# Sums of q's squares by column-group products, the last values turned a unit later, and selection matrices made in the unit before

## The chip, the cores and the metric

The kernel runs on one core of a Trainium2 chip. The metric is the time on the device in microseconds (us), lower is better. A core has TensorE (PE; its weight loads are listed as PEld), VectorE (DVE), ScalarE (ACT), GpSimd (POOL) and SyncE (SP), which here issues most transfers. Each engine works through its own instructions in order; where one needs a result of another engine it waits on a semaphore, and everything behind it on that engine waits with it.

## The reference

A trunk of two layers over 512 positions and 1024 channels in float32. Layer 0 mixes by a gated DeltaNet (8 heads of 128), layer 1 by a Conformer convolution; each layer then attends to a memory of 256 rows and goes through a squared-ReLU MLP. The parts that matter here:

```python
def l2_normalize(x):
    return x * lax.rsqrt(jnp.sum(x * x, axis=-1, keepdims=True) + 1e-6)

def gated_deltanet(h, w_in, w_conv, a_log, dt_bias, out_norm, w_out):
    proj = h @ w_in
    qkv = jax.nn.silu(causal_depthwise_conv(qkv, w_conv))   # q, k, v of 8 heads
    ...
    q = l2_normalize(q) * (DN_HEAD_DIM ** -0.5)
    k = l2_normalize(k)
    ...
    o = chunk_gated_delta_rule(q, k, v, g, beta)
    o = o * lax.rsqrt(jnp.mean(o * o, axis=-1, keepdims=True) + RMS_EPS) * out_norm
    o = o * jax.nn.silu(z)
    return o @ w_out

def conformer_conv(h, w_pw1, b_pw1, w_dw, b_dw, ln_g, ln_b, w_pw2, b_pw2):
    u = h @ w_pw1 + b_pw1
    u = u[..., :D_MODEL] * jax.nn.sigmoid(u[..., D_MODEL:])
    c = causal_depthwise_conv(u, w_dw) + b_dw
    c = jax.nn.silu(layer_norm(c, ln_g, ln_b))
    return c @ w_pw2 + b_pw2
```

For each head and position the sum of q's 128 squares is needed. It enters only in the normalization of the output, so it may come late.

## The kernel before

Activations lie with 128 channels on the partitions and 512 positions along the row. A float32 weight is held as a rounded high part and a rest: ScalarE casts the loaded `raw` to `wh` (L253), VectorE subtracts to get `wl` (L73), and a product is three matmuls (L300 to L302: wh with xh, wh with xl, wl with xh). A projection tile of 128 output channels and 512 positions is 24 matmuls.

The DeltaNet part is written as a row of units: `mains` has the projections, two units for a tile, in the order k, q, z, v of heads 0 to 3 (group 0), then the same of heads 4 to 7 (group 1), then the keys and values of the memory (K and V in the names). Beside it stands a table: `S.at(unit, rank, f, ...)` puts the work f into a unit, and ranks order the work of one unit. Tables at the end of the file give the units: `Q3` for q's squares of each head, `FS` for the recursion on X. The framework's scheduler makes each engine's order from these instructions as they are written out, so a change of a table moves instructions of several engines against each other.

Names in the profile: `h` is a projection's PSUM tile; v0 to v7 in the text are the tiles of the eight heads' values. `cv` is VectorE's copy of such a tile out of PSUM (scaled by `rb`), `cva` the result of the short convolution; q of head h ends as such a `cva` in `QT[h]`, 128 channels x 512 positions. `X` and `fst` are the steps of the recursion that inverts the triangular matrices, all on VectorE, with widths such as 9x23 = 207; it ends with a 32x32 transpose of X to `UB`, copies from UB to `u` and transposes of u to `x`. `mss` and `msd` belong to the memory's norm.

The sums of q's squares: `q3` (L671, L674) turns q of one head by four TensorE transposes into PSUM (`qt`), so that positions lie on the partitions, and ScalarE squares each 128x128 block with a running sum into one column of `ssq` (an ACTIVATE and a READ_ACCUMULATOR each); `norm_q` then adds epsilon.

The values: `v2` turns the values of a group by transposes (`vt`, L818). In group 1, heads 0 to 2 are turned in one unit and head 3 in the next.

The Conformer: `mlp7` (the MLP of layer 0) ends with the residual sums `h`, from which the next norm takes high and low parts `xh` (ACT) and `xl` (DVE) and squares `sq`, summed on GpSimd and VectorE in two accumulators. The conformer's first products `pw` use xh and xl; `ssq` there is the sum of the squares by a product with ones, issued in unit `STAT` of the pw loop. VectorE makes three selection matrices `sel` (L1420 to L1422) at the conformer's start.

Of the kernel before, what the change touches and what calls it, by code (L numbers as in the profile page):

```python
# [10 lines left out]
AF = mybir.ActivationFunctionType  # L11
ALU = mybir.AluOpType
AX = mybir.AxisListType

P = 128
NT = 512
NTAP = 4
PH = 16
KT = 8
EPS = 1e-6  # L20
# [18 lines left out]
def tile_trunk(ctx, tc, xT, memT, x_d, mem_d, prm_d, adt_d, bdw_d, tap_d, fin_d, first_d, w_ab, w_kq, w_v, w_z, w_dno, w_pw1, w_pw2,  # L39
               w_q, w_k, w_vv, w_o, w_up, w_dn, yT):  # L40
    nc = tc.nc
    pe, act, dve, pool = nc.tensor, nc.scalar, nc.vector, nc.gpsimd
# [15 lines left out]
    def slot(dt=F32, s="u", shape=(P, NT)):  # L58
        return up.tile(list(shape), dt, tag="u", name=nm(s))

    def psum(s="ps"):
        return psp.tile([P, NT], F32, tag="ps", name=nm(s))
# [4 lines left out]
    def const(shape, s, dt=F32):  # L67
        return cp.tile(list(shape), dt, tag=s, name=s)
# [3 lines left out]
    def tt(e, o, a, b, op):  # L72
        r = e.tensor_tensor(out=o, in0=a, in1=b, op=op)  # L73
        if e is pool:
            last_pool[:] = [r]
        return r
# [4 lines left out]
    def ts(e, o, a, s1, op0, s2=None, op1=None):  # L81
        if op1 is None:
            return e.tensor_scalar(out=o, in0=a, scalar1=s1, scalar2=None, op0=op0)
        return e.tensor_scalar(out=o, in0=a, scalar1=s1, scalar2=s2, op0=op0, op1=op1)

    def c4(t):
        return t.rearrange("p (c i) -> p c i", c=4)
# [4 lines left out]
    def over_c(t, n=4):  # L92
        return t.unsqueeze(1).to_broadcast([P, n, t.shape[1]])
# [18 lines left out]
    def piece(e, i):  # L112
        e.dma_start(out=raw0[:, i * 256:(i + 1) * 256], in_=w_kq[0][:, i * 256:(i + 1) * 256])
# [11 lines left out]
    ident = const([P, P], "ident")  # L125
# [4 lines left out]
    for i in range(WARM):  # L130
# [5 lines left out]
    pool.affine_select(out=tri_gt, in_=ones, pattern=[[-1, P]], compare_op=ALU.is_gt, fill=0.0,  # L136
                       base=0, channel_multiplier=1)
    piece(act, 1)
    ones_r = const([P, P], "ones_r", F32R)
    pool.tensor_copy(ones_r, ones)  # L140
    tri_mid = const([P, P], "tri_mid")
# [58 lines left out]
    for kind, gq in DN_ORDER:  # L200
        for i in range(2):
            j = gq * 2 + i
# [202 lines left out]

    class Norm:
        def __init__(self, gname):
            self.g, self.acc, self.xs, self.n, self.side = gname, None, [], 0, None

        def add(self, t, h):  # L410
            self.parts(t, h)
# [6 lines left out]
            pin(stt(xl, h, pc(self.g, t), xh.bitcast(F32), ALU.mult, ALU.subtract))  # L418
            self.xs.append((xh, xl))

        def square(self, h, e=pool, side=False):
            sq = slot(s="sq")
            act.activation(sq, h, AF.Square)  # L423
            self.n += 1
            if side:
                if self.side:
                    tt(pool, self.side, self.side, sq, ALU.add)
                self.side = self.side or sq
                return
            if self.acc is None:  # L430
                self.acc = sq
            else:
                tt(dve if self.n == KT else e, self.acc, self.acc, sq, ALU.add)
            if self.n == KT:
                if self.side:
                    tt(dve, self.acc, self.acc, self.side, ALU.add)
                self.hl = split(self.acc, "sq")

        def stat(self):
# [28 lines left out]
    class DeltaNet:  # L468
# [196 lines left out]
            self.QT[h] = qT  # L665

        def q3(self, h):
            ps, sq = psum("qt"), slot(s="sqq")
            for c in range(4):
                cs = slice(c * P, (c + 1) * P)  # L670
                pe.transpose(ps[:, cs], self.QT[h][:, cs], ident)  # L671
            for c in range(4):
                cs = slice(c * P, (c + 1) * P)
                act.activation(sq[:, cs], ps[:, cs], AF.Square, accum_out=self.ssq[:, 4 * h + c:4 * h + c + 1])  # L674

        def norm_q(self, gq):
            v = self.ssq[:, 16 * gq:16 * gq + 16]
            ts(dve, v, v, EPS, ALU.add, EPS * P, ALU.mult)


        def fs_in(self, h):
# [291 lines left out]
    def mem_gain(layer, half):  # L973
        gn = f"xa_mem{layer}"
        if half == 0:
            mem["xs"] = []
        for j in (2 * half, 2 * half + 1):
            if layer == 1:
                m = mem["m"][j].rearrange("p (k t) -> p k t", k=2)
                tt(dve, m, m, over_c(mem["rs"][:, 0:256], 2), ALU.mult)  # L980
            mh = slot(F32R, "mh")
            ml = slot(F32R, "ml")
            for i in range(2):
                ks = slice(i * 256, (i + 1) * 256)
                src = mem["m"][j][:, ks]
                g = pc(gn, 2 * j + i)
                act.activation(mh[:, ks], src, AF.Copy, scale=g)
                stt(ml[:, ks], src, g, mh[:, ks].bitcast(F32), ALU.mult, ALU.subtract)
                mem["xs"].append((mh[:, ks], ml[:, ks]))
# [176 lines left out]
    def mlp7(layer, norm, hres, nxt=None, mid=None):  # L1166
# [123 lines left out]
        new = [None] * 8  # L1290

        def outs(tiles):
            todo = [(n, c, i) for n in range(2) for c in range(2) for i in tiles]
            pss = {i: psum("hT") for i in tiles}
            for n, c, i in todo:
                j = 2 * n + c
                pe.transpose(pss[i][:, j * P:(j + 1) * P], acc[n, 1 - i // 4, c][:, i % 4 * P:i % 4 * P + P], ident)
            for k, i in enumerate(tiles):
                hn = slot(s="h")
                tt(dve, hn, pss[i], hres[i], ALU.add)  # L1300
                new[i] = hn
                if k:
                    nxt.parts(i - 1, new[i - 1])
                if i > 5:
                    nxt.square(new[i - 2], side=True)
            nxt.parts(i, hn)
            for hn in new[0:4] if i == 3 else new[6:8]:
                nxt.square(hn, pool if i == 3 else dve)

        def final(n, m, c, held=None):  # L1310
            opens = n not in fin or fin[n][4][c] is None
# [62 lines left out]
        for g in range(4):  # L1374
            ops, us = [{} for _ in range(4)], []
            for i in range(8):
                w = wnext(("up", layer, g * 4 + i // 2), i % 2)
                ps = psum("up")
# [25 lines left out]
    def taps(m, *pieces):  # L1404
        TAPS.setdefault(m, [])
        for i in pieces:
            t = slot(s="tap")
            nc.sync.dma_start(out=t, in_=tap_d[m - NTAP, i])
            TAPS[m].append(t)

    def conformer(norm, hres, nxt, rest):
        xs = norm.xs
        st, x16 = {}, {}
# [2 lines left out]
        Yp = [fsp.tile([P, 1024], F32, tag="fs", name=nm("cyp")) for _ in range(2)]  # L1416
        bias = slot(s="bdw")[:, 0:P]
        nc.sync.dma_start(out=bias, in_=bdw_d)
        sel = slot(s="sel")
        dve.tensor_reduce(out=sel[:, 128:160], in_=ident.rearrange("p (g t) -> p t g", g=4), op=ALU.add, axis=AX.X)  # L1420
        dve.tensor_reduce(out=sel[:, 160:164], in_=c4(ident), op=ALU.add, axis=AX.X)
        dve.tensor_copy(c4(sel[:, 0:128]), over_c(sel[:, 128:160]))  # L1422
        own, same_t = over_c(sel[:, 160:164]), sel[:, 0:128]

        def pw_mm(i, hf):
# [242 lines left out]
        new = []  # L1668
# [4 lines left out]
        for m in range(8):  # L1673
            w, ps = pss[m] if m in pss else (wnext(("pw2", m // 2), m % 2), psum("pw2"))
            proj(w, ss, ps, 4 if m in pss else 0)
            hn = slot(s="h")
# [13 lines left out]
    for i in range(4):  # L1690
        s = slice(i * 256, (i + 1) * 256)
# [30 lines left out]
    D = DeltaNet(n0)  # L1722
    D.decay_const(0)
    mains, S = [], Sides()
# [70 lines left out]
    for gq in range(2):  # L1795
        f0, nf = FS[gq]
        S.at(f0, 5, D.fs_begin, gq)
        for i in range(nf):
            S.at(f0 + i, 6, D.fs_steps, gq, i * 31 // nf, (i + 1) * 31 // nf)
        S.at(f0 + nf, 1, D.fs_end, gq)  # L1800
        for h in range(4 * gq, 4 * gq + 4):
            S.at(f0 + nf, 1, D.mg_a, h)
        S.at(f0 + 1, 7, D.norm_k, gq)
        S.at(f0 + nf + 2, 7, D.norm_q, gq)
        for i in range(4):
            h = 4 * gq + i
            S.at(f0 + nf - 4 + i, 5, D.mg_pre, h)
        a, b = (4 * gq, 4 * gq + 1), (4 * gq + 2, 4 * gq + 3)
        for j, (f, x, y) in enumerate(((D.mg_wy, a, ()), (D.mg_wy, b, a), (D.mg_te, a, ()), (D.mg_te, b, a), (D.mg_te, (), b))):
            S.at(MG[gq] + j, 1, f, x, y)  # L1810
        S.at(MG[gq] + 2, 1, D.mg_wy, (), b)
        for j, x in ((1, a), (2, b)):
            S.at(MG[gq] + j, 1.5, D.mg_u, x)
        for c in range(4):
            u = at["v", 4 * gq + 3] + V2[gq]
            if gq == 1:
                S.at(u, 3, D.v2, gq, c, (0, 1, 2))
                S.at(u + 1, 0, D.v2, gq, c, (3,))
        n = 0
        for c in range(4):  # L1820
            for step in range(3):
                S.at(REC[gq] + n, 0, D.rec, gq, c, step)
                n += 1
            S.at(REC[gq] + n + (c < 3 if gq == 1 else -(c == 1)), 5, D.o_gate, gq, c)
        S.at(ONORM[gq], 1, D.o_norm, gq)
    S.at(MSQ - 4, 7, mem_tok)
    for j in range(4):
        S.at(MSQ + j, 7, mem_square, j)
# [33 lines left out]
    h = []  # L1862
# [12 lines left out]
    n2 = Norm("mlp_norm0")  # L1875
    h = xattn(0, n1, h, n2)
    n3 = Norm("cv_norm")
    h, rest = mlp7(0, n2, h, n3, lambda: (mem_gain(1, 0), mem_gain(1, 1), taps(NTAP, *range(9))))
    n4 = Norm("xa_norm1")
    h = conformer(n3, h, n4, rest)  # L1880
    n5 = Norm("mlp_norm1")
# [3 lines left out]
    mlp7(1, n5, h)  # L1885


NSLOT = 69
NCV = 6
NRAW = 3  # L1890
RAWB = 6
# [21 lines left out]
ROOT_K = (32, 72)  # L1913
K2 = (15, 16, 18, 19, 45, 46, 49, 48)
Q2 = (18, 20, 22, 23, 48, 50, 50, 53)
Q3 = (24, 25, 27, 29, 55, 56, 57, 59)
FS = ((22, 9), (52, 8))
MG = (36, 68)
V2 = (10, 9)
# [6 lines left out]
TAPK = {0: 8, 1: 9, 2: 11, 3: 12}  # L1926
TAPQ = {0: 12, 4: 44}
TAPV = (37, 38, 39, 40, 69, 69, 70, 71)
STAT = 2
TAPS_U = (4,) * 7 + (6,) * 9 + (3,) * 8 + (0,) * 8  # L1930
TAPS_C = {4: 0, 5: 0, 6: 0, 7: 0}
SHARE = 5
# [113 lines left out]
```

## Time and profile before

| what | us |
|---|---|
| median of 3 runs (1444.5 to 1446.05) | 1444.7 |
| the profiled execution | 1444.54 |
| its span | 1442.8 |
| PE busy | 1432.4 |
| DVE busy | 1053.5 |
| ACT busy | 763.6 |
| POOL busy | 249.2 |

The profiled execution takes 1.7 us more than its span, which runs from its first to its last instruction. The core's mean granted TensorE clock was 0.999. A row of a timeline has the start in us, the duration in us, engine, line, operation, output and inputs, and in brackets the engine's idle time before it and what released it. TensorE's durations are modelled, and neighbours overlap: what a matmul costs the stream is the distance between the starts.

### The profile page before, as it was taken

The page shows a single profiled execution, that of the slowest core. Times are in us where ns is not written, and L with a number is a line of the kernel's source. Part 1 is how long each engine was busy: PE and PEld are TensorE (multiplying, and loading weights), DVE is VectorE, ACT ScalarE, POOL GpSimd, SP SyncE. Part 2 cuts the span into 40 slices and gives each one's busy share as a digit, 9 for nine tenths or more (in the row PEclk, how much of TensorE's full clock was granted, in tenths as well). Part 3 has the DMA queues.
Part 4 walks back from the last instruction along what each step waited for, and adds up shares of the span by engine and source line. Part 5 has one row for each costly group of instructions (what it writes and reads, how often), then busy time and mean ns, then how long its engine had stood idle before and what let it go on. Part 6 is the DMA issues. An engine that isn't in the chain of part 4 may idle for free.

```text
span 1442.8 us, 20243 instructions
## 1 busy us (share of the span) xinstructions
PE 1432.4 (99%) x7670; PEld 1199.2 (83%) x7670; DVE 1053.5 (73%) x1600; ACT 763.6 (53%) x1322; POOL 249.2 (17%) x250
## 2 busy tenths in 40 slices
PE   9999999999999999999999999999999999999998
PEld 7888889888888888888888778888888888888886
DVE  6989888867555765767679899975555766767677
ACT  6767856655444454434355655564444544444354
POOL 1301200102113010010100478111112010010101
PEclk9999999999999999999999999999999999999999
DMA  8232225522214576575766448743215476675853
GB/s 300 73 117 75 70 92 162 195 84 88 74 40 127 153 177 175 141 206 131 198 165 217 141 147 244 252 139 99 73 49 141 117 182 169 149 206 135 222 150 88
DMA packets 71857, 207.80 MB, mean 144 GB/s; under 512 B 15440, under 2 KB 16592, under 8 KB 71760
## 3 DMA queue, kind: packets, MB, share of 16 engines
q1 hardware_dynamic: 60960, 169.22, 35.9%
q0 software_dynamic: 9792, 35.66, 14.5%
q10 hardware_dynamic: 1008, 1.64, 0.3%
q8 instruction: 60, 0.98, 0.3%
q14 instruction: 37, 0.30, 0.1%
HBM read 203.28 MB, written 3.21 MB: 143 GB/s over the span
## 4 chain that ended last, share of the span: by engine, by line
PE 91%; DVE 5%; ACT 2%; issue 1%; DMA 0%; POOL 0%; SPq 0%; DVEq 0%; ACTq 0%; POOLq 0%
PE up L302 8%; PE up L301 8%; PE up L300 8%; PE dn L1218 7%; PE dn L1217 7%; PE dn L1216 7%; PE h L300 3%; PE h L302 3%; PE h L301 3%; PE xo L301 2%; PE q L301 2%; PE xo L300 2%; PE q L300 2%; PE q L302 2%; PE xo L302 2%; PE pw L302 2%
## 5 line engine op out<-in xcount | busy, mean ns | idle before, releaser
L253 ACT CAST wh<-raw 128x1024 fp32r<-128x1024 f32 x259 | 271.6, 1051 | 345.0 <-issue 89.1
L73 DVE TENSOR_TENSOR wl<-raw,wh 128x1024 fp32r<-128x1024 f32 (+1 forms) x250 | 306.0, 1225 | 97.1 <-ACT wh L253 94.8
L300 PE MATMUL up<-xh,wh 128*128 128x512 f32 x512 | 199.7, 390 | 0.0
L302 PE MATMUL up<-xh,wl 128*128 128x512 f32 x512 | 199.3, 389 | 0.0
L301 PE MATMUL up<-xl,wh 128*128 128x512 f32 x512 | 199.2, 389 | 0.0
L302 PEld LDWEIGHTS up<-xh,wl 128*128 128x128 f32 x512 | 96.1, 188 | 19.9
L300 PEld LDWEIGHTS up<-xh,wh 128*128 128x128 f32 x512 | 96.1, 188 | 19.9
L301 PEld LDWEIGHTS up<-xl,wh 128*128 128x128 f32 x512 | 96.1, 188 | 19.9
L241 POOL DMA_DIRECT2D t<-w_dn x48 | 42.1, 914 | 367.5 <-DVE wl L73 269.6
L1216 PE MATMUL dn<-wh,ah 128*128 128x512 f32 (+1 forms) x260 | 100.5, 387 | 0.0
L1218 PE MATMUL dn<-wl,ah 128*128 128x512 f32 (+1 forms) x260 | 100.4, 386 | 0.0
L1217 PE MATMUL dn<-wh,al 128*128 128x512 f32 (+1 forms) x260 | 100.4, 386 | 0.0
L79 DVE SCALAR_TENSOR_TENSOR rl<-up,rb 128x512 f32<-128x512 f32 x64 | 44.1, 689 | 58.4 <-PE up L302 58.4
L253 ACT CAST wh<-t 128x1024 fp32r<-128x1024 f32 x44 | 46.4, 1054 | 55.0 <-PE dn L1217 43.7
L73 DVE TENSOR_TENSOR wl<-t,wh 128x1024 fp32r<-128x1024 f32 x44 | 53.6, 1223 | 28.7 <-ACT wh L253 28.6
L73 POOL TENSOR_TENSOR sq<-sq,sq 128x512 f32<-128x512 f32 x28 | 46.0, 1643 | 154.2 <-ACT sq L423 143.6
L1495 DVE SCALAR_TENSOR_TENSOR ca<-xn,prm,ca 128x512 f32<-128x512 f32 x85 | 64.1, 754 | 5.7 <-ACT ca L1492 3.4
L73 DVE TENSOR_TENSOR acc<-acc,dn 128x512 f32<-128x512 f32 x99 | 66.6, 682 | 1.0
L300 PE MATMUL h<-xh,wh 128*128 128x512 f32 x160 | 64.2, 401 | 0.0
L302 PE MATMUL h<-xh,wl 128*128 128x512 f32 x160 | 62.5, 390 | 0.0
L301 PE MATMUL h<-xl,wh 128*128 128x512 f32 x160 | 62.4, 390 | 0.0
L73 DVE TENSOR_TENSOR al<-u,ah 128x512 fp32r<-128x512 f32 x64 | 44.1, 688 | 21.4 <-ACT ah L359 21.4
(421 smaller groups left out, 3520.2 us busy)
## 6 DMA issues: line engine op xcount, KB each, us to landing
raw<-w_dn SPq DMA_DIRECT2D x68, 512.0 KB, 4.5
raw<-w_up SPq DMA_DIRECT2D x64, 512.0 KB, 4.8
t<-w_dn POOLq DMA_DIRECT2D x48, 512.0 KB, 6.4
tap<-tap SPq DMA_DIRECT2D x48, 256.0 KB, 6.2
raw<-w_pw SPq DMA_DIRECT2D x24, 512.0 KB, 4.6
raw<-w_dn POOLq DMA_DIRECT2D x20, 512.0 KB, 6.6
raw<-w_k SPq DMA_DIRECT2D x16, 512.0 KB, 4.1
raw<-w_vv SPq DMA_DIRECT2D x16, 512.0 KB, 6.1
```

Of the source, the lines that this page charges most:

```text
L73: r = e.tensor_tensor(out=o, in0=a, in1=b, op=op)
L79: return dve.scalar_tensor_tensor(out=o, in0=a, scalar=s, in1=b, op0=op0, op1=op1)
L241: nc.gpsimd.dma_start(out=t, in_=a, accum_op=ALU.add)
L253: ins = [act.copy(h, raw)]
L300: pe.matmul(ps, wh, xh, start=first, stop=False)
L301: pe.matmul(ps, wh, xl, start=False, stop=False)
L302: pe.matmul(ps, wl, xh, start=False, stop=last)
L1216: pe.matmul(ps, xh, w[0][:, s], start=opens and k == 0, stop=False, skip_group_check=True)
L1217: pe.matmul(ps, xl, w[0][:, s], start=False, stop=False, skip_group_check=True)
L1218: pe.matmul(ps, xh, w[1][:, s], start=False, stop=k == 3, skip_group_check=True)
L1495: first["tap"] = dve.scalar_tensor_tensor(out=a, in0=src, scalar=w, in1=a, op0=ALU.mult, op1=ALU.add)
```

## The change

Four edits.

1. **q's squares.** `q3` now only squares q of a head on ScalarE, 128x512 at once, without turning it. `q_sums` multiplies the squares of the four heads of a group by a constant `selq` of 32 columns (ones and zeros) into the four 32-row groups of one PSUM tile `qq`. Group 0's tile is copied to SBUF by ScalarE, and VectorE adds group 1's to it. `q_turn` then turns this one tile by four transposes and writes `ssq` with two VectorE instructions, epsilon included. `norm_q` goes. `Q3` has other units, and there are `QS` for q_sums and `QS[1] + 2` for q_turn. Two memsets on GpSimd make selq at the start.
2. **Values.** In group 1, head 3 is turned two units after the other heads' unit instead of one.
3. **Selection matrices.** The three `sel` instructions move from the conformer's start into the middle of the MLP before it.
4. **Squares of the conformer's norm.** One accumulator instead of two: three squares are taken in the middle and five at the end, with two additions on GpSimd and five on VectorE; `ssq` is issued one step later (`STAT` 3).

```diff
+    selq = const([P, 48], "selq")
+    pool.memset(selq, 1.0)
+    pool.memset(selq[:, 16:32], 0.0)
...
-            for hn in new[0:4] if i == 3 else new[6:8]:
-                nxt.square(hn, pool if i == 3 else dve)
+            for k in range(3) if i == 3 else range(3, 8):
+                nxt.square(new[k], pool if i == 3 else dve)
...
         def q3(self, h):
-            ps, sq = psum("qt"), slot(s="sqq")
-            for c in range(4):
-                cs = slice(c * P, (c + 1) * P)
-                pe.transpose(ps[:, cs], self.QT[h][:, cs], ident)
-            for c in range(4):
-                cs = slice(c * P, (c + 1) * P)
-                act.activation(sq[:, cs], ps[:, cs], AF.Square, accum_out=self.ssq[:, 4 * h + c:4 * h + c + 1])
-
-        def norm_q(self, gq):
-            v = self.ssq[:, 16 * gq:16 * gq + 16]
-            ts(dve, v, v, EPS, ALU.add, EPS * P, ALU.mult)
+            sq = self.M["sq", h] = slot(s="sqq")
+            act.activation(sq, self.QT[h], AF.Square)
+
+        def q_sums(self, gq):
+            ps = psum("qq")
+            for j in range(4):
+                pe.matmul(ps[32 * j:32 * j + 32, :], selq[:, 16 * gq:16 * gq + 32], self.M.pop(("sq", 4 * gq + j)),
+                          start=True, stop=True)
+            if gq == 0:
+                self.qq = slot(s="qq")
+                act.copy(self.qq, ps)
+            else:
+                tt(dve, self.qq, self.qq, ps, ALU.add)
+
+        def q_turn(self):
+            ps = psum("qt")
+            for c in range(4):
+                cs = slice(c * P, (c + 1) * P)
+                pe.transpose(ps[:, cs], self.qq[:, cs], ident)
+            v = self.ssq.rearrange("p (g j c) -> p g j c", g=2, j=4)
+            for gq in range(2):
+                ts(dve, v[:, gq], ps.rearrange("p (c j g x) -> p g j c x", c=4, j=4, g=2)[:, gq, :, :, 0],
+                   EPS, ALU.add, EPS * P, ALU.mult)
...
+    def selections():
+        sel = slot(s="sel")
+        dve.tensor_reduce(out=sel[:, 128:160], in_=ident.rearrange("p (g t) -> p t g", g=4), op=ALU.add, axis=AX.X)
+        dve.tensor_reduce(out=sel[:, 160:164], in_=c4(ident), op=ALU.add, axis=AX.X)
+        dve.tensor_copy(c4(sel[:, 0:128]), over_c(sel[:, 128:160]))
+        SEL.append(sel)
...
-        S.at(f0 + nf + 2, 7, D.norm_q, gq)
+        S.at(QS[gq], 3, D.q_sums, gq)
...
-                S.at(u + 1, 0, D.v2, gq, c, (3,))
+                S.at(u + 2, 0, D.v2, gq, c, (3,))
...
+    S.at(QS[1] + 2, 3, D.q_turn)
...
-    h, rest = mlp7(0, n2, h, n3, lambda: (mem_gain(1, 0), mem_gain(1, 1), taps(NTAP, *range(9))))
+    h, rest = mlp7(0, n2, h, n3, lambda: (mem_gain(1, 0), mem_gain(1, 1), taps(NTAP, *range(9)), selections()))
...
-Q3 = (24, 25, 27, 29, 55, 56, 57, 59)
+Q3 = (27, 28, 28, 29, 56, 57, 58, 59)
+QS = (30, 60)
...
-STAT = 2
+STAT = 3
```

How this moves instructions is seen in each engine's order. A row has the line in its own file, the operation, output and inputs with their buffer numbers, and in brackets the engines or transfers that it waits for. Three places follow.

**TensorE at the end of v6** (its tile is h_2555 in the kernel before, h_2506 in the changed one; the next is v7). Before:

```order
L300 MATMUL h_2555<-xh_173,wh_2419 128x512
L301 MATMUL h_2555<-xl_175,wh_2419 128x512
L302 MATMUL h_2555<-xh_173,wl_2420 128x512
L300 MATMUL h_2590<-xh_138,wh_2491 128x512 [waits Activation_49]
L301 MATMUL h_2590<-xl_140,wh_2491 128x512
L302 MATMUL h_2590<-xh_138,wl_2492 128x512 [waits DVE_49]
```

In the changed kernel:

```order
L303 MATMUL h_2506<-xh_176,wh_2370 128x512
L304 MATMUL h_2506<-xl_178,wh_2370 128x512
L305 MATMUL h_2506<-xh_176,wl_2371 128x512
L670 MATMUL qq_2479<-sqq_2387,selq 32x512 [waits Activation_49]
L670 MATMUL qq_2479<-sqq_2415,selq 32x512 [waits Activation_49]
L682 MATMUL qt_2519<-ident,qq_1133 128x128 [waits DVE_49]
L682 MATMUL qt_2519<-ident,qq_1133 128x128 x3
L303 MATMUL h_2547<-xh_141,wh_2436 128x512
L304 MATMUL h_2547<-xl_143,wh_2436 128x512
```

Two products and the four transposes of qq stand between v6 and v7. The group's other two products stand alone, one after 12 matmuls of v5, one after the first matmul of v6. In group 0, three products stand after 12 matmuls of v2 and the fourth 9 matmuls later.

**VectorE behind v6.** Before (cv_2581 is the copy of v6):

```order
L73 TENSOR_TENSOR X_2142<-X_2142,fst_2414 128x9x23 [waits DVE_49]
L73 TENSOR_TENSOR cv_2581<-h_2555,rb_318 128x512 [waits PE_49]
L73 TENSOR_TENSOR fst_2438<-FT_2145,X_2142 128x192 [waits DVE_49]
L73 TENSOR_TENSOR wl_2587<-raw_2489,wh_2586 128x1024 [waits DMAHW3_49,Activation_49]
L73 TENSOR_TENSOR X_2142<-X_2142,fst_2438 128x8x24 [waits DVE_49]
```

In the changed kernel these twelve rows follow the copy of v6, cv_2538:

```order
L73 TENSOR_TENSOR X_2119<-X_2119,fst_2365 128x9x23 [waits DVE_49]
L73 TENSOR_TENSOR fst_2391<-FT_2122,X_2119 128x192 [waits DVE_49]
L73 TENSOR_TENSOR wl_2544<-raw_2434,wh_2543 128x1024 [waits DMAHW3_49,Activation_49]
L73 TENSOR_TENSOR X_2119<-X_2119,fst_2391 128x8x24 [waits DVE_49]
L73 TENSOR_TENSOR fst_2394<-FT_2122,X_2119 128x175 [waits DVE_49]
L73 TENSOR_TENSOR X_2119<-X_2119,fst_2394 128x7x25 [waits DVE_49]
L73 TENSOR_TENSOR fst_2397<-FT_2122,X_2119 128x156 [waits DVE_49]
L73 TENSOR_TENSOR X_2119<-X_2119,fst_2397 128x6x26 [waits DVE_49]
L73 TENSOR_TENSOR fst_2400<-FT_2122,X_2119 128x135 [waits DVE_49]
L73 TENSOR_TENSOR X_2119<-X_2119,fst_2400 128x5x27 [waits DVE_49]
L73 TENSOR_TENSOR fst_2422<-FT_2122,X_2119 128x112 [waits DVE_49,PE_49]
L73 TENSOR_TENSOR qq_1133<-qq_1133,qq_2479 128x512 [waits PE_49]
```

The X step of 207 (9x23) moved behind the copy, and the sum of qq stands behind the step fst of width 112. On ScalarE, the fourth square of the group, sqq_2415, stands right behind CAST wh_2543, which waits for TensorE. The two weights that came later among these steps before, wl_2579 the first of them in the changed kernel, now stand behind UB's transpose, the copies to u and the transposes to x.

**VectorE and ScalarE at mss and the fourth square of group 0.** VectorE before (cv_1123 is the copy of v1):

```order
L73 TENSOR_TENSOR cv_1123<-h_1073,rb_318 128x512 [waits PE_49]
L73 TENSOR_TENSOR fst_1060<-FT_869,X_866 128x247 [waits DVE_49]
L73 TENSOR_TENSOR wl_1141<-raw_998,wh_1140 128x1024 [waits DMAHW2_49,Activation_49]
L73 TENSOR_TENSOR X_866<-X_866,fst_1060 128x13x19 [waits DVE_49]
L73 TENSOR_TENSOR mss_880<-mss_880 128x2
```

VectorE in the changed kernel:

```order
L73 TENSOR_TENSOR cv_1094<-h_1048,rb_321 128x512 [waits PE_49]
L73 TENSOR_TENSOR fst_1067<-FT_872,X_869 128x231 [waits DVE_49]
L73 TENSOR_TENSOR X_869<-X_869,fst_1067 128x11x21 [waits DVE_49]
L73 TENSOR_TENSOR wl_1112<-raw_981,wh_1111 128x1024 [waits DMAHW2_49,Activation_49]
L73 TENSOR_TENSOR fst_1070<-FT_872,X_869 128x220 [waits DVE_49]
L73 TENSOR_TENSOR mss_883<-mss_883 128x2
```

ScalarE in the changed kernel (before, msd stood in the same place and the blocks of the fourth head behind it and the second table load):

```order
L665 ACTIVATE sqq_1063<-cva_632 128x512
L256 CAST wh_1111<-raw_981 128x1024 [waits DMAHW2_49,DVE_49,PE_49]
L971 ACT_TABLE_LOAD
L971 ACTIVATE msd_1209<-mss_883,eps_rms 128x2 [waits DVE_49]
L665 ACTIVATE sqq_1092<-cva_697 128x512
L817 ACTIVATE nk<-sek 128x16
L819 ACT_TABLE_LOAD
```

mss stood behind the X step of 13x19 and now stands behind fst of width 220, five X and fst steps later; the fourth square stands behind msd, which waits for mss.

More of the change, by code (lines that the diff above doesn't have):

```diff
@@ L407, in __init__ @@
         def __init__(self, gname):
-            self.g, self.acc, self.xs, self.n, self.side = gname, None, [], 0, None
+            self.g, self.acc, self.xs, self.n = gname, None, [], 0
         def add(self, t, h):
@@ L419, in parts, with square @@
             self.xs.append((xh, xl))
-        def square(self, h, e=pool, side=False):
+        def square(self, h, e=pool):
             sq = slot(s="sq")
@@ L424, in square @@
             self.n += 1
[L425 to L429, printed above, removed]
             if self.acc is None:
@@ L434, in square @@
             if self.n == KT:
-                if self.side:
-                    tt(dve, self.acc, self.acc, self.side, ALU.add)
                 self.hl = split(self.acc, "sq")
@@ L1303, in outs @@
                     nxt.parts(i - 1, new[i - 1])
-                if i > 5:
-                    nxt.square(new[i - 2], side=True)
             nxt.parts(i, hn)
-            for hn in new[0:4] if i == 3 else new[6:8]:
-                nxt.square(hn, pool if i == 3 else dve)
+            for k in range(3) if i == 3 else range(3, 8):
+                nxt.square(new[k], pool if i == 3 else dve)
         def final(n, m, c, held=None):
@@ L1409, in taps @@
             TAPS[m].append(t)
+    SEL = []
+    def selections():
[4 more added lines that the diff above has]
+        SEL.append(sel)
     def conformer(norm, hres, nxt, rest):
@@ L1418, in conformer @@
         nc.sync.dma_start(out=bias, in_=bdw_d)
[L1419 to L1422, printed above, removed]
+        sel = SEL[0]
         own, same_t = over_c(sel[:, 160:164]), sel[:, 0:128]
@@ L1885, in tile_trunk @@
     mlp7(1, n5, h)
-NSLOT = 69
+NSLOT = 70
 NCV = 6
```

## The prediction

> **What bounds the kernel now.** The page's first table and its chain of work come first.
>
> ```profile
> PE 1432.4 (99%) x7670; PEld 1199.2 (83%) x7670; DVE 1053.5 (73%) x1600; ACT 763.6 (53%) x1322; POOL 249.2 (17%) x250
> ...
> PE 91%; DVE 5%; ACT 2%; issue 1%; DMA 0%; POOL 0%; SPq 0%; DVEq 0%; ACTq 0%; POOLq 0%
> ```
>
> TensorE is busy in all but some 10 us and is 91% of the chain. So time that is taken off or put onto TensorE, as work or as waiting, goes to the end one for one unless a later wait swallows it. The next question is where the little idle time lies, which the busy time by stretches tells (columns: stretch, its length, PE busy, granted clock, DMA share, GB/s).
>
> ```profile
> 20.00:250.00 230.00, 230.00 (x1616) 1.00 0.35 111
> 250.00:270.00 20.00, 19.45 (x169) 1.00 0.35 111
> ...
> 785.00:800.00 15.00, 14.04 (x69) 1.00 0.34 110
> ```
>
> The squares of q are turned between 84 and 216 us (a row below), in a stretch with no idle time at all: no gap there can take new work. The late values lie in 250 to 270 (0.55 us idle), the conformer's start in 785 to 800 (0.96).
>
> **What the q part removes.** Rows of TensorE's timeline around the first removed block, and the group of all of them:
>
> ```profile
> 83.78 0.39 PE L353 MATMUL z<-wl,xh 128*128 128x512 f32 x1
> 84.01 0.40 PE L354 MATMUL z<-wh,xl 128*128 128x512 f32 x1
> 84.25 0.60 PE L671 MATMUL qt<-ident,cva 128*128 128x128 f32 x4
> ...
> 84.92 0.40 PE L353 MATMUL z<-wl,xh 128*128 128x512 f32 x1
> ...
> L671 PE MATMUL qt<-ident,cva x32: 270/272/275, 84.2 to 215.7; 128*128 128x128 f32 x32
> ```
>
> A dense matmul takes its pitch, 84.01 − 83.78 = 0.23 us. From 84.01 to 84.92 there are 0.91 us for two pitches and the block, so four transposes cost 0.91 − 0.46 = 0.45. Of 32 there are 8 blocks: **−3.6 us**, −1.8 in each group of heads. ScalarE loses its 64 short instructions; it is not on the path there, so that is costed at nothing.
>
> **What it adds.** Products into 32-column groups are in the kernel already, in the first projection:
>
> ```profile
> 12.86 0.51 PE L1740 MATMUL h<-xl,wh 128*128 128x512 f32 x1
> 13.30 1.06 PE L1744 MATMUL ab<-x,abp 128*32 128x512 f32 x8
> ...
> 14.64 0.40 PE L1739 MATMUL h<-xh,wl 128*128 128x512 f32 x1
> ...
> L1744 PE MATMUL ab<-x,abp x16: 592/604/617, 10.6 to 13.8; 128*32 128x512 f32 x16
> ```
>
> Each f32 product is two pieces of 0.60. Eight pieces, four products into four different column groups, end within 1.06, so pieces of different groups run beside each other; what the clump costs the stream is 14.64 − 12.86 − 2 × 0.23 = 1.32. A single product still has two pieces one after the other, so I take 1.32 for a clump of one to four: the nearest row, an upper bound for fewer. The lower bound of a lone product is two dense pitches, 0.45. The change pays off only with its four products side by side. The order breaks them into 3 and 1 in group 0, and into 1, 1 and 2 in group 1: five clumps instead of two, 6.6 us rather than 2.6.
>
> The Trainium skill's page TensorEngine Tiling (Array Packing), section Tiling Modes, says that column tiles work independently and that switching the tiling mode drains TensorE. The trace agrees with the first (eight pieces in 1.06); the 0.26 between 1.32 and 1.06 may be the drain. Its Overview promises up to four times the speed at 32 columns; if a lone product had that too, the sum would be the second rival's.
>
> **Group 0: a new wait.** The fourth product waits for sqq_1092, which now stands on ScalarE behind msd, which waits for VectorE's mss; and mss stands five steps of the X recursion later than before.
>
> ```profile
> 99.63 0.48 PE L300 MATMUL h<-xh,wh 128*128 128x512 f32 x1
> ...
> 102.09 0.15 DVE L73 TENSOR_TENSOR mss<-mss 128x2 f32<-128x2 f32 x1
> 102.21 0.41 DVE L73 TENSOR_TENSOR fst<-FT,X 128x240 f32<-128x240 f32 x1
> ...
> 104.27 0.16 DVE L965 RECIPROCAL mtok<-msd 128x2 f32<-128x2 f32 x1
> ...
> 102.28 0.30 ACT L963 ACTIVATE msd<-mss,eps_rms 128x2 f32<-128x2 f32 x1 [0.69 <-DVE mss L73]
> 102.48 0.20 ACT L809 ACTIVATE nk<-sek 128x16 f32<-128x16 f32 x1
> ...
> L423 ACT ACTIVATE sq<-h x40: 612/617/625, 330.7 to 1106.8; 128x512 f32<-128x512 f32 x40
> ```
>
> The five steps take 104.27 − 102.21 = 2.06, so msd starts at about 102.28 + 2.06 = 104.34, the square 0.20 later, and it ends 0.62 after that, at 105.16. On TensorE v2 starts 1.8 earlier than 99.63, at 97.83; 12 matmuls (2.72), the clump of three (1.32) and 9 matmuls (2.04) bring it to 103.9. It waits 1.3 us. Group 0: −1.8 + 1.3 + 1.3 + 1.3 = **+2.1** (if mss comes in time and products cost 0.45 each: −0.9).
>
> **Group 1: the turn before v7.** At the end of v6 there are two products, then the transposes of qq, which wait for VectorE's add, then all of v7. Rows of before around the end of v6 (226.72 is v7's first matmul):
>
> ```profile
> 226.10 0.37 DVE L73 TENSOR_TENSOR X<-X,fst 128x207 f32<-128x207 f32 x1
> 226.92 0.69 DVE L73 TENSOR_TENSOR cv<-h,rb 128x512 f32<-128x512 f32 x1 [0.45 <-PE h L302]
> ...
> 231.45 0.28 DVE L73 TENSOR_TENSOR fst<-FT,X 128x112 f32<-128x112 f32 x1
> ...
> 226.69 1.05 ACT L253 CAST wh<-raw 128x1024 fp32r<-128x1024 f32 x1 [4.38 <-PE h L301]
> 227.66 0.26 ACT L674 ACTIVATE sqq<-qt 128x128 f32<-128x128 f32 x1
> ...
> 226.72 0.39 PE L300 MATMUL h<-xh,wh 128*128 128x512 f32 x1
> ```
>
> VectorE's cv waits for v6's end and had been idle 0.45 us for it, so nothing behind it can be done earlier. From v6's end to the end of fst 128x112 pass 231.73 − 226.72 = 5.0 us; the X step of 207, now behind cv, adds 0.37. Only then comes the add of qq, which reads PSUM as cv does and takes as long: 0.69. So the sum is ready some 6.1 after v6's end. The products themselves are not the limit: the CAST ahead of the fourth square also waits for v6's end, the square starts 0.97 after it (227.66 − 226.69), takes 0.62, and its product is done at 2.9. TensorE then stands for over 3 us. With the turn's own 0.45, v7 starts **6.5 us** after v6's end instead of at once. The two lone products in v5 and v6 add 2.6: group 1 gives −1.8 + 2.6 + 6.5 = **+7.3** (lone products at 0.45: +5.6). Queued behind the waiting transposes are v7 and all key products, whose inputs are ready: a pure loss.
>
> After that VectorE has its lateness to make up. Rows of before on what follows there, and the pitch of key products:
>
> ```profile
> 235.11 1.25 DVE L711 STREAM_TRANSPOSE UB<-X 128x1024 f32<-128x1024 f32 x1
> ...
> 243.48 1.18 DVE L73 TENSOR_TENSOR wl<-raw,wh 128x1024 fp32r<-128x1024 f32 x1
> ...
> 232.16 0.28 PE L300 MATMUL K<-mh,wh 128*128 128x256 f32 x1
> 232.28 0.28 PE L301 MATMUL K<-ml,wh 128*128 128x256 f32 x1
> ```
>
> Before, 235.11 − 231.73 = 3.4 us passed from fst 128x112 to UB's transpose, less a cv and a weight (0.69, 1.18) 1.5; from there to 243.48 it was 8.4, less two weights 6.0. Now these stand without the weights: 6.1 + 1.5 + 6.0 = 13.6 after v6's end, then cv of v7 and wl_2579 make it 15.5. TensorE asks for wl_2579 after v7 (232.16 − 226.72 = 5.4) and two key tiles (48 × 0.12 = 5.8), at 6.5 + 11.2 = 17.7. Two us of cover; without it the third key tile waits.
>
> SyncE's two early w_vv loads now stand behind two t loads that wait for buffers:
>
> ```profile
> 237.87 4.21 SPq L234 DMA_DIRECT2D t<-w_dn x2
> ...
> L352 PE MATMUL V<-wh,mh x32: 389/393/477, 261.3 to 292.8; 128*128 128x512 f32 x32
> ```
>
> They start at about 242 (237.87 + 4.21), 19 us ahead of their use: nothing. Two memsets on GpSimd (17% busy), one ScalarE copy and two tiny VectorE instructions lie beside other work.
>
> **Values of head 3 turned later.**
>
> ```profile
> PE vt L818 <- ACT cva L613: 0.6, 1, 0.6
> ```
>
> That is the total of the wait, its count and the longest in us. A unit later it goes: −0.7 with the restart (0 to −1.0).
>
> **Conformer.** Weight loads that waited for xl, and the three sel instructions that leave this place for the MLP before it:
>
> ```profile
> 798.62 0.19 PEld L301 LDWEIGHTS pw<-xl,wh 128*128 128x128 f32 x1 [1.08 <-DVE xl L79]
> 799.88 0.19 PEld L301 LDWEIGHTS pw<-xl,wh 128*128 128x128 f32 x1 [0.73 <-DVE xl L79]
> 801.14 0.19 PEld L301 LDWEIGHTS pw<-xl,wh 128*128 128x128 f32 x1 [0.27 <-DVE xl L79]
> 802.85 0.19 PEld L301 LDWEIGHTS pw<-xl,wh 128*128 128x128 f32 x1 [0.50 <-DVE xl L79]
> ...
> 794.03 0.38 DVE L1420 TENSOR_REDUCE sel<-ident 128x32 f32<-128x128 f32 x1
> ...
> 795.26 1.28 DVE L73 TENSOR_TENSOR h<-hT,h 128x512 f32<-128x512 f32 x2
> ```
>
> The waits sum to 2.58. VectorE gets 795.26 − 794.03 = 1.23 earlier to h and xl, so I take −1.5, between nothing and −2.6. Two more VectorE adds of squares come after the last xl; they hide behind the products, since ssq is asked for three matmuls later.
>
> **The sum.** +2.1 + 7.3 − 0.7 − 1.5 = +7.2 on the profiled execution's 1444.54; that lies 0.16 below the median of 1444.7, so **1451.9**. Low bounds together: −0.9 + 5.6 − 1.0 − 2.6 = +1.1 (1445.8); high: +2.1 + 7.3 and 2 for wl_2579 with nothing gained, +11.4 (1456).
>
> **Rivals.** (1) *VectorE stays late* and wl_2579 is late for the third key tile: 1453 to 1456. For: VectorE has a chain without a pause and 2 us of cover; against: the copies and turns took no longer in the rows. It decides once VectorE loses 2 us more. Chance 0.10. (2) *A lone product costs a quarter of a clump*, 0.25. Group 0 still ends by the late square, (105.2 + 0.25 + 0.68) − 105.2 = +0.9; group 1 is −1.8 + 0.5 + 6.5 = +5.2; with −2.2, 1448.6. Against: two pieces of one product use the same columns. 0.12. (3) *Everything small*: products near 0.45, no late mss, the conformer's waits all gone: the low bounds, within 0.2%, 0.10. (4) *The turn finds its sum ready*, the faster side: at the turn, VectorE reaches the add as soon as the products end. With products at 0.25 and no wait the sum is −3.6 + 2.0 + 0.45 − 0.7 − 2.6 = −4.4, 1440.3; it decides as soon as v7 starts no more than about 2.5 us after v6's end. Against it: 5.4 us of VectorE work behind an instruction that cannot start before v6's end. 0.05. My forecast has 0.63.
>
> About 0.2% (2.9 us, 1441.8 to 1447.6) is what a measurement here can tell from no change. Faster by more: 0.06 (rival 4 and a little); within: 0.13 (rival 3 and the edge of 2); slower: 0.81. The range, 1446.0 to 1455.0, leaves out rival 4 and the ends of 1 and 3.
>
> **What would show it.** The page after should have TensorE idle for the first time between 20 and 250: a row of the transposes of qq that waits over 3 us for VectorE's add, and one of the fourth product of group 0 that waits about 1 for ScalarE. Rows of qq alone between dense matmuls should push the next start by over 1 us; a push of 0.3 would speak for rival 2. The wait of vt should be gone and those of pw down to a third. I am wrong if v7 starts within 4 us of v6's end, or if the idle time stays at 10 us.

## The result and the profile after

The changed kernel takes 1453.07 us (median of 4 runs, 1452.55 to 1453.52) against 1445.27 for the kernel before in the same job: ratio 1.0054, 95% interval 1.0036 to 1.0071. It is slower by 7.8 us. The profiled execution took 1452.87, 8.3 more than that of before (1444.54), with a span of 1451.2.

The same views as before, of the changed kernel: busy time, the chain by engine, then the longest waits of TensorE (total, count, longest in us), then its busy time by stretches.

```profile
PE 1437.6 (99%) x7658; PEld 1199.1 (83%) x7658; DVE 1052.8 (73%) x1603; ACT 760.1 (52%) x1267; POOL 245.3 (17%) x250
...
PE 87%; DVE 8%; DMA 2%; ACT 2%; issue 1%; POOL 1%; SPq 0%; ACTq 0%; DVEq 0%; POOLq 0%
...
PE qt L682 <- DVE qq L73: 3.6, 1, 3.6
...
PE qq L670 <- ACT sqq L665: 1.2, 2, 0.7
...
100.00:115.00 15.00, 14.30 (x62) 1.00 0.23 74
222.00:240.00 18.00, 13.89 (x45) 0.81 0.34 107
```

Two things in the page contradict each other at first sight: TensorE has 12 matmul records fewer and yet 5 us more of busy time. The last row tells half of it: in 222 to 240 its granted clock is 0.81 on average, and matmuls there take longer (some 2.4 us, below). The other half is that five clumps of products at about 1.2 us each and the turn add more than the eight blocks of transposes took off. The waits of vt and of pw for xl that stood among the longest before are gone; two new ones, both on q's sums, have come.

TensorE's timeline at the end of v6 shows both parts of the loss:

```profile
227.93 0.39 PE L305 MATMUL h<-xh,wl 128*128 128x512 f32 x1
228.25 1.04 PE L670 MATMUL qq<-sqq,selq 128*32 128x512 f32 x2
229.75 1.05 PE L670 MATMUL qq<-sqq,selq 128*32 128x512 f32 x2 [0.46 <-ACT sqq L665]
234.45 1.11 PE L682 MATMUL qt<-ident,qq 128*128 128x128 f32 x4 [3.65 <-DVE qq L73]
235.21 0.78 PE L303 MATMUL h<-xh,wh 128*128 128x512 f32 x1
235.78 0.63 PE L304 MATMUL h<-xl,wh 128*128 128x512 f32 x1
236.21 0.63 PE L305 MATMUL h<-xh,wl 128*128 128x512 f32 x1
...
242.77 0.28 PE L303 MATMUL K<-mh,wh 128*128 128x256 f32 x1
```

First the waits: 0.46 us for the square, then 3.65 for VectorE's sum. Then v7 itself: its matmuls follow each other at 236.21 − 235.78 = 0.43 us instead of 0.23, until about 239.5. From its first matmul to the first key product it takes 242.77 − 235.21 = 7.56 us; before it took 5.44. The clock in short stretches there (same columns as before):

```profile
232.00:232.50 0.50, 0.00 (x0) 1.00 0.63 156
232.50:233.00 0.50, 0.00 (x0) 0.63 0.95 303
233.00:233.50 0.50, 0.00 (x0) 0.50 0.94 238
...
239.00:239.50 0.50, 0.50 (x2) 0.54 0.74 197
239.50:240.00 0.50, 0.50 (x3) 1.00 0.71 287
...
235.00:240.00 5.00, 5.00 (x15) 0.55 0.51 157
```

While TensorE stands still, its granted clock falls to half at about 232.6 (a mean of 0.63 in that stretch), and it comes back at about 239.46, 5 us after TensorE has started again. VectorE's rows give the wait its cause:

```profile
228.35 0.69 DVE L73 TENSOR_TENSOR cv<-h,rb 128x512 f32<-128x512 f32 x1 [2.04 <-PE h L305]
...
233.52 0.28 DVE L73 TENSOR_TENSOR fst<-FT,X 128x112 f32<-128x112 f32 x1
233.71 0.68 DVE L73 TENSOR_TENSOR qq<-qq,qq 128x512 f32<-128x512 f32 x1
```

VectorE stood idle 2.04 us for v6, then worked for five microseconds on v6's copy, X steps and one weight, and then did the sum for which TensorE waited. Group 0's wait, on VectorE, ScalarE and TensorE in turn:

```profile
103.37 0.15 DVE L73 TENSOR_TENSOR mss<-mss 128x2 f32<-128x2 f32 x1
...
103.56 0.30 ACT L971 ACTIVATE msd<-mss,eps_rms 128x2 f32<-128x2 f32 x1 [3.65 <-DVE mss L73]
103.76 0.61 ACT L665 ACTIVATE sqq<-cva 128x512 f32<-128x512 f32 x1
...
104.43 1.04 PE L670 MATMUL qq<-sqq,selq 128*32 128x512 f32 x2 [0.70 <-ACT sqq L665]
```

The same matmuls can be found in both traces, so the difference can be cut into stages, each from one such matmul to another:

| stage | forecast | profiled executions |
|---|---|---|
| third z half to the first vt (group 0) | +2.1 | 75.05 → 76.22: +1.2 |
| first vt to the first key tile (group 1) | +7.3 | 89.32 → 99.00: +9.7 |
| last key tile to the first vn behind the late vt | −0.7 | 13.71 → 13.00: −0.7 |
| last MLP tile to the first depthwise tile (conformer) | −1.5 | 65.19 → 63.40: −1.8 |
| sum | +7.2 | +8.4 |

### The profile page after: what moved, and what is told of

Its sections match the earlier page's. It is cut to its first block, busy times and chain, and to the rows that moved or that the text cites. A ratio compares the mean times of both kernels' runs of the same rounds, so it can differ in the third digit from the quotient of the medians.

```text
span 1451.2 us, 20173 instructions
## 1 busy us (share of the span) xinstructions
PE 1437.6 (99%) x7658; PEld 1199.1 (83%) x7658; DVE 1052.8 (73%) x1603; ACT 760.1 (52%) x1267; POOL 245.3 (17%) x250
## 4 chain that ended last, share of the span: by engine, by line
PE 87%; DVE 8%; DMA 2%; ACT 2%; issue 1%; POOL 1%; SPq 0%; ACTq 0%; DVEq 0%; POOLq 0%
PE up L303 8%; PE up L305 8%; PE up L304 8%; PE dn L1226 7%; PE dn L1224 7%; PE dn L1225 7%; PE pw L304 2%; PE pw L303 2%; PE pw L305 2%; PE xo L304 2%; PE q L304 2%; PE xo L303 2%; PE q L305 2%; PE q L303 2%; PE xo L305 2%; PE h L303 2%
## 5 line engine op out<-in xcount | busy, mean ns | idle before, releaser
L73 POOL TENSOR_TENSOR sq<-sq,sq 128x512 f32<-128x512 f32 x26 | 42.8, 1647 | 151.5 <-ACT sq L426 137.3
```

## The experiments

Ratios are against the kernel before, run in the same job, with 95% intervals; stages are those of the table, read off each kernel's profile. In several executions the time ahead of the first stage differs by up to 1.3 us (TensorE waits 0.4 to 0.8 us for the first norm in some and not at all in others); the stages leave that out. The stage of group 0 also ends with small matmuls of the recursion's merge (`mg`), whose part varies by itself: from the first of them to the first vt it took 23.96 us before, and 24.52 and 23.95 in two profiles of one kernel (edits 2 to 4). Up to the first mg these profiles agree: 51.09 in all three.

**Edits 2 to 4 alone, and edit 1 alone.** The first is the kernel before with the late values, the earlier selection matrices and the regrouped squares; the second has only what the diff does to q.

> The kernel before with edits 2 to 4 alone (values later, selection matrices earlier, squares regrouped); q's squares as before. My theory, that edit by edit the gains read off the changed kernel's trace (0.7 for the values, 1.8 for the conformer) belong to these edits: 2.5 us faster than before, about 1442.7, no wait of vt, and pw waiting for xl about 0.5 in all. Rival, that they only showed because q's part had made everything later: at most 1 us faster, 1444 or more.

> The kernel before with q's part alone (edit 1). My theory: all of the loss is here, 10.5 us slower than before (1.2 in group 0, 9.4 in group 1), about 1455.6, with TensorE 3.6 us idle ahead of the transposes of qq and v7 at half clock behind them. Rival, that the edits hang together and the values' wait is swallowed by q's delay: the wait of vt vanishes here too, and it is 9.8 slower or less.

Edits 2 to 4: 1443.53 against 1445.21, ratio 0.9985 (0.9975 to 0.9995); by stages −0.7 for the values and −1.7 for the conformer, with no wait of vt left, and +0.6 in group 0, all of it in the merge and absent from the same kernel's second profile. Edit 1: 1456.0, ratio 1.0068 (1.0053 to 1.0083); by stages +1.4 in group 0, +9.6 in group 1, and nothing in the other two (13.70 and 65.16, with the wait of vt back at 0.6). The edits add up: +10.8 and −1.7 make +9.1 in the medians beside 7.8 measured, and without that +0.6 the stages make +10.9 and −2.4, +8.5 beside 8.4. The rival by which the gains only came of q's delay (at most 1 us faster) falls: both gains stand in the stages here, and a second timing of the same kernel, below, gives 2.6 us.

**The products side by side, the turn later.** The changed kernel with these lines of the table changed:

```diff
-QS = (30, 60)
+QS = (33, 65)
-    S.at(QS[1] + 2, 3, D.q_turn)
+    S.at(69, 3, D.q_turn)
```

> The changed kernel with QS = (33, 65) and the turn in unit 69: all four products of a group stand side by side, and the turn stands among the merge's products, behind its sum. My theory, that the place and not the method costs the time: TensorE's q work is 2 x 1.2 + 0.45 = 2.9 instead of 3.6, no wait for qq, clock 1.00 throughout, so with edits 2 to 4 about 1445.0 - 0.7 - 2.5 = 1441.8. Rival, that the sum on VectorE makes the recursion late and TensorE waits for the merge's inputs instead: 1445 to 1448, with an idle row at mg or K between 235 and 260.

> Edits 2 to 4 alone, timed once more beside the version with the products together. By the traces so far 0.7 for the values and 1.7 for the conformer are gone, so about 2 us faster than before.

> The products together and the turn in unit 69, timed once more on the same chip as edits 2 to 4 alone. My theory: TensorE's q work is 2 x 1.2 + 0.4 = 2.8 instead of 8 x 0.45 = 3.6, so 0.8 us below edits 2 to 4 alone, some 3 us faster than before. Rival, that the method gives nothing over the transposes: the two agree within 0.4 us.

First job: 1442.39, ratio 0.9979 (0.9969 to 0.9989). Second job: 1442.16, ratio 0.9976 (0.9966 to 0.9985), beside 1442.84 and 0.9982 (0.9973 to 0.9991) for edits 2 to 4 alone. TensorE's clump of four, and its busy time and clock over the whole stage, in the second job's profile:

```profile
108.45 0.39 PE L305 MATMUL h<-xh,wl 128*128 128x512 f32 x1
108.77 1.07 PE L670 MATMUL qq<-sqq,selq 128*32 128x512 f32 x8
...
110.10 0.39 PE L304 MATMUL h<-xl,wh 128*128 128x512 f32 x1
...
20.00:250.00 230.00, 230.00 (x1613) 1.00 0.34 112
```

Four products push the stream by 110.10 − 108.45 − 2 × 0.23 = 1.19 us, no more than one alone does, and no idle time is left. So the method is sound and its place was the trouble. Against edits 2 to 4 alone of the same job the stages differ by −0.7 in group 0 up to the merge (50.38 and 51.09), −0.8 in group 1 up to the keys (88.50 and 89.32), +0.5 among the keys, where the turn now stands, and +0.1 behind them, −0.9 in all; the first job's profiles have the same two gains (50.39 and 51.09, 88.51 and 89.33). The medians differ by 1.1 in the first job and 0.7 in the second. The intervals against before overlap, but both jobs and both pairs of profiles point the same way, to about what the sum says (2.8 against 3.6).

**The turn behind v7, products where they were.** Only the turn's unit changes, 62 to 64:

> The changed kernel with the turn two units later (unit 64); the products stay in their units and come out as 3 and 1 in group 0 and as four lone products in group 1, the last two inside v7, and the turn stands behind v7. My theory splits the loss into the standing still at the turn with its half clock (about 6 us) and the lone products (five clumps at 1.2 where two would do, 3.6): with the first gone, about 1453.1 - 6.0 = 1447, clock 1.00, each lone product still pushing the stream by 1.2. Rival, that a lone product is cheap when it stands in the stream and only those at v6's end were dear: 1444 to 1445.

1447.95, ratio 1.0021 (1.0011 to 1.0030). From the first vt to the keys 92.91, 6.1 less than in the changed kernel. The clock stays at 1.00 from 222 to 240. Lone products in v7, as this timeline shows, push the stream as far as four do:

```profile
228.94 0.39 PE L305 MATMUL h<-xh,wl 128*128 128x512 f32 x1
...
230.57 0.39 PE L304 MATMUL h<-xl,wh 128*128 128x512 f32 x1
...
234.45 0.39 PE L303 MATMUL h<-xh,wh 128*128 128x512 f32 x1
234.77 1.04 PE L670 MATMUL qq<-sqq,selq 128*32 128x512 f32 x2
235.75 0.50 PE L304 MATMUL h<-xl,wh 128*128 128x512 f32 x1
236.08 0.40 PE L305 MATMUL h<-xh,wl 128*128 128x512 f32 x1
```

At 234.77 the push is 236.08 − 234.45 − 2 × 0.23 = 1.17; at 228.94 it is 1.17 too. So some 6 us of the loss were the standing still with its clock. The rest above the version side by side, 1447.95 against 1442.4, is products in pieces and the wait of group 0: by stages 3.9 in group 1 (92.91 less 88.50 and less the turn's 0.5, which here lies ahead of the keys) and 1.9 in group 0 up to the merge (52.25 and 50.38), of which the wait is 0.59. The rival with cheap lone products falls.

**The wait filled with work that nobody needs.** The changed kernel with 28 transposes of one square, written to a PSUM tile that is not read, ahead of the turn; then with 14. (q_sums also keeps the squares, which it gave up before.)

```diff
         def q_turn(self):
+            fill = psum("fill")
+            for c in range(28):
+                pe.transpose(fill[:, 0:P], self.M["sq", 7][:, 0:P], ident)
             ps = psum("qt")
```

> The changed kernel with 28 transposes of one square, whose result is read by nothing, between the last product and the turn: TensorE works through most of the wait for VectorE's sum, which stays. My theory, that v7 ran at half clock because TensorE had stood idle: the granted clock stays 1.00, v7 takes 5.4 us instead of 7.6, the turn 0.45 instead of 0.76, and the time is 2.4 below the changed kernel, about 1450.6. Rival, that v7 is slow for another reason (transfers at that place take 0.86 of the DMA engines' time): v7 keeps its pitch of 0.43 us and the time stays at 1453.

> As the fill run, with 14 transposes instead of 28: TensorE is idle for about 2 us ahead of the turn instead of 0.4 (fill) or 3.65 (changed kernel). If the clock falls only after more than 3 us of standing still, it stays at 1.00 and v7 takes 5.4 us, about 1451. If less is enough, v7 starts at half clock and takes 7.6, about 1453.

With 28: 1451.2, ratio 1.0034 (1.0021 to 1.0047), and 2.4 less from the first vt to the keys than in the changed kernel (96.63). With 14, timed once: 1450.71, and 96.64 to the keys. TensorE's rows at the turn and its busy time, clock and transfers in v7, first with 28, then with 14:

```profile
232.00 3.27 PE L681 MATMUL fill<-ident,sqq 128*128 128x128 f32 x28
235.72 0.66 PE L685 MATMUL qt<-ident,qq 128*128 128x128 f32 x4 [0.44 <-DVE qq L73]
236.13 0.48 PE L303 MATMUL h<-xh,wh 128*128 128x512 f32 x1
236.45 0.40 PE L304 MATMUL h<-xl,wh 128*128 128x512 f32 x1
236.68 0.39 PE L305 MATMUL h<-xh,wl 128*128 128x512 f32 x1
...
236.00:241.00 5.00, 5.00 (x26) 1.00 0.48 147
```

```profile
230.87 1.75 PE L681 MATMUL fill<-ident,sqq 128*128 128x128 f32 x14
234.60 0.66 PE L685 MATMUL qt<-ident,qq 128*128 128x128 f32 x4 [1.98 <-DVE qq L73]
235.01 0.48 PE L303 MATMUL h<-xh,wh 128*128 128x512 f32 x1
235.32 0.40 PE L304 MATMUL h<-xl,wh 128*128 128x512 f32 x1
235.56 0.39 PE L305 MATMUL h<-xh,wl 128*128 128x512 f32 x1
...
232.00:234.00 2.00, 0.62 (x6) 1.00 0.71 240
```

In both, the turn comes no sooner after v6: it starts 6.3 us behind v6's end in all three kernels. But the turn then takes 0.41 us instead of 0.76, and v7 runs at its usual pitch, with 14 too, where TensorE still stands 1.98 us and the clock stays at 1.00. The transfers beside v7 are the same: the DMA engines' share is 0.48 here and 0.51 in the changed kernel (235 to 240). So the slow v7 came of the clock. That useless work made the kernel faster is shown by the stage, 96.63 and 96.64 against 99.00 (98.88 in edit 1 alone); the two ratios against before have intervals that overlap.

The wait's length alone does not decide. In the changed kernel the clock fell 1.8 us after TensorE's last product had ended, and here 1.98 us of standing brought no fall. What lay ahead differs: dense transposes here, and there 2.6 us with only two products on 32 columns and a short wait. Which of these counts was not tried.

**The conformer's gain, edit by edit.**

> The kernel before with the selection matrices alone made earlier (edit 3). My theory, that VectorE's 1.2 us ahead of the first h and xl are most of the conformer's gain: 1.2 faster, pw waiting for xl some 1.3 in all. Rival, that the wait is set by xl running slowly beside GpSimd's additions: 0.3 or less.

> The kernel before with the squares regrouped and asked for a step later alone (edit 4). My theory: 0.6 faster, since GpSimd has no additions beside the fourth xl, which took 1.83 instead of 0.75. Rival, that this edit brings nearly all of the conformer's 1.8, and the selection matrices nothing.

Selection matrices alone: ratio 0.9996 (0.9986 to 1.0005), the conformer's stage 64.71 instead of 65.19. Squares and STAT alone: 0.9996 (0.9987 to 1.0005), 63.73. Neither differs from before in the timing; the split rests on one profile of each. By it, −0.5 and −1.5: my expectation (1.2 and 0.6) had it the wrong way round. VectorE's xl and GpSimd's additions beside them, before, then with the matrices moved, then with the squares regrouped:

```profile
796.74 1.83 DVE L79 SCALAR_TENSOR_TENSOR xl<-h,prm,xh 128x512 fp32r<-128x512 f32 x1 [0.19 <-ACT xh L416]
...
800.35 2.44 DVE L79 SCALAR_TENSOR_TENSOR xl<-h,prm,xh 128x512 fp32r<-128x512 f32 x2
...
793.27 4.75 POOL L73 TENSOR_TENSOR sq<-sq,sq 128x512 f32<-128x512 f32 x3
800.52 1.73 POOL L73 TENSOR_TENSOR sq<-sq,sq 128x512 f32<-128x512 f32 x1 [2.50 <-ACT sq L423]
```

```profile
796.82 1.01 DVE L79 SCALAR_TENSOR_TENSOR xl<-h,prm,xh 128x512 fp32r<-128x512 f32 x1 [0.19 <-ACT xh L416]
...
800.06 2.24 DVE L79 SCALAR_TENSOR_TENSOR xl<-h,prm,xh 128x512 fp32r<-128x512 f32 x2
```

```profile
797.14 0.75 DVE L79 SCALAR_TENSOR_TENSOR xl<-h,prm,xh 128x512 fp32r<-128x512 f32 x1 [0.20 <-ACT xh L416]
...
799.67 1.63 DVE L79 SCALAR_TENSOR_TENSOR xl<-h,prm,xh 128x512 fp32r<-128x512 f32 x2
...
793.67 3.36 POOL L73 TENSOR_TENSOR sq<-sq,sq 128x512 f32<-128x512 f32 x2
```

Before, two additions of GpSimd lay beside xl: the xl at 796.74 took 1.83 instead of 0.75, the last two 2.44 instead of 1.6. Moving the matrices brings VectorE there earlier, but GpSimd is still adding, and the last pair is nearly as slow as before. With two additions fewer on GpSimd, none is left beside xl, though the matrices still stand in the way. That the additions slow xl is read from the rows lying side by side, here in three kernels; the additions alone were not taken away.

## Why the prediction held, and where it was off

- **TensorE as the bound.** Right: the four stages add up to +8.4 and the span grew by 8.4. Nothing was swallowed on the way.
- **What is removed.** Right: each block was worth 0.45; up to v2 of the changed kernel its four blocks had brought 1.8.
- **What is added.** Right in kind: five clumps, each pushing the stream alike whether it holds one product or four. The size is 1.17 to 1.25 where 1.32 was taken: in the rows of that reading the matmul ahead of the clump itself lasts 0.51 instead of 0.39, and this 0.12 was put down to the clump. Four of the five clumps are terms of the sum (the fifth lies within the wait of the turn); they make 0.5 us less.
- **Group 0's wait.** The mechanism was right, mss late and the fourth square behind it, the size half: 0.70 instead of 1.3. The term mis-sized is the start of the five steps. It was taken from VectorE's times of before, but there VectorE had stood 0.73 us idle for a weight, which no longer happens, so all its later steps come earlier and mss is 1.3 us later than before instead of 2.1. The row of before:

```profile
85.75 1.23 DVE L73 TENSOR_TENSOR wl<-raw,wh 128x1024 fp32r<-128x1024 f32 x1 [0.73 <-ACT wh L253]
```

- **The turn before v7.** Right, and the largest term: the sum was ready 234.39 − 228.16 = 6.2 us after v6's end (228.16 is the last matmul's start and a pitch), where 6.1 was forecast.
- **v7 after the turn.** This step was missing. v7 was counted at 5.4 us and the turn at 0.45; standing still took the clock to half, and they took 7.56 and 0.76: 2.4 us, which the run with 28 transposes gave back. The Trainium skill has this on its page TensorE: Matmul & The Clock Gate, section Part 1: The HAM clock gate: an idle window of about 3.4 us halves the clock, and about as long a busy one restores it. The trace agrees that standing still halves the clock and that full work restores it, but not on the times counted from the standing still: here the clock fell 1.8 us after the last product's end and came back 5.0 us after TensorE had started again.
- **VectorE's lateness afterwards.** Right: no key tile waited. But the 2 us of cover were not put to the test: v7 at half clock gave VectorE 2 us more.
- **Values.** Right, −0.7. **Conformer.** Right in size, −1.8 for −1.5, for half a reason: the forecast put the gain on the earlier selection matrices, and the profiles put most of it (−1.5 alone, against −0.5) on the regrouped squares.
- **The four rivals.** The turn did not find its sum ready; lone products were not cheap; VectorE's lateness cost nothing more. The low bounds together would have needed cheap lone products and mss in time, and neither came.

That the forecast of +7.2 lies within 1.2 us of the stages' +8.4 is in part luck: the missing clock (+2.4) was partly balanced by clumps and a wait that were taken too dear (−0.5, and −0.6 in group 0).

## What to carry to other kernels

When small products go to column groups, count the clumps in the order of issue and not the products: one alone costs the stream what four side by side cost. An instruction on the bounding engine that needs the result of an engine working through its own chain belongs behind the work that does not need it; three numbers of a table decided here between +7.8 and −3.3 us. Where TensorE cannot help waiting, look at its clock behind the wait as well as at the wait.

## What the runs showed of the hardware that was not expected

- The granted clock fell to 0.50 within a wait of 3.65 us, 1.8 us after TensorE's last work (which 0.46 of waiting and a product on 32 columns preceded), and came back 5.0 us after the work began again. In edit 1 alone it fell 1.7 us after the last product and came back after 4.8. At half it stayed 6.8 us in both. A wait of 1.98 behind dense transposes left it at 1.00.
- One product of 32 columns and four of them in different column groups take the same 1.04 to 1.07 us; both push the stream by 1.17 to 1.25.
- Half of the transposes' filling (1.75 us of work) was as good as all of it (3.27 us): 96.64 and 96.63 from the first vt to the keys.
